# One-hot matrices in the place of one weight slot, row transposes done later, and outputs stored by halves of the tokens

## The chip, the cores and the metric

The kernel runs on one core of a Trainium2 chip. The metric is the time of one execution in device microseconds (us); lower is better. Engines are named as the profile names them: PE (TensorE matmuls), PEld (TensorE weight loads), DVE (VectorE), ACT (ScalarE), POOL (GpSimd), SP (the queue that issues the weight transfers). A small q behind a name means the engine's sequencer.

## The reference, cut to what matters

Two layers of a diffusion backbone on 256 latent and 256 context tokens of width 1024. After its mixer each layer has a mixture of experts: a router picks 2 of 16 experts for every token, and the experts' results come back to their tokens, weighted by the gates:

```
idx, gates = route(tokens, router_w, router_b)          # 2 of 16 experts a token
for e in range(16):                                     # SwiGLU, 1024 -> 768 -> 1024
    y_e = (silu(h[tok_e] @ w_gate[e]) * (h[tok_e] @ w_up[e])) @ w_down[e]
    y[tok_e] += gate_e * y_e
x = layer_norm(alpha * x + m[5] * y)
```

Layer 0 does this for all 512 tokens, layer 1 for the 256 latent ones. The weights of one expert are 9.4 MB in float32 and are read from DRAM for each layer, 16 experts times 2 layers. The output is the latent stream, 256 x 1024.

## The kernel before

Activations lie feature-major in SBUF (128 partitions x 8 feature tiles x tokens). A residual sum `acc` (`self.acc`) takes every sub-layer's result; the layer norm of the next stage reads it.

**Weights and slots.** Expert weights come in chunks of 1536 KB: four for gate and up (`gu`, from `in_egu`) and two for down (`ed`, from `in_ed`), six an expert. A chunk lands in a slot of 12 KB a partition. Layer 0's experts have ten slots: three of `ring`, four in `big`, three of `more` (`R1, R2, R3`, L39; `open_slots`, L1448). `wload` (L334) takes the slot at the head of a list and puts it back at the tail, so load number n takes the slot that load n-10 had, and SP issues it when PE has made its last use of that one. The order of loads is gu(0), then gu(e), ed(e-1) for e from 1 on. Two slots are also held until the first gather of tokens has been issued (`self.held`, L1458).

**The expert loop** (L1766) runs over e from 0 to 15; p = e // 2 is the pair, m = e % 2. Step e puts on PE, in this order: `hidden` of expert e (`gu0p` in the trace: 128 matmul instructions for the first 64 tokens, one run-time branch each for tokens 65 to 96 and 97 to 128), for odd e the `features` of the next pair (`xt0p`), then `down` of expert e-1 (`dp0p`). PE's own order is kept as written (`self.pin`), except for the blocks under a run-time branch (`when`, L1488). The results of both experts of a pair are put in one tile Y.

**How results come back to the tokens in layer 0.** There are two ways. Pairs 0 to 5 (`NS = 6`) scatter their rows to DRAM (`scatter`, L1600, on POOL): four planes, one for each 256 features, with two rows a token, one for each of its two experts. When pair 5 is scattered, at e = 12, `fetch(0)` (L1612) reads the rows of the 256 context tokens back on POOL's queue in 16 transfers into a tile `rows0` and adds the two rows of each token on POOL, in two halves of 128 tokens (L1620). `collect(got, 0)` (L1624) transposes these rows on PE (16 matrices of 128 x 128, `cl` in the trace), and DVE adds them to `acc` (8 instructions, L1597). `fetch(1)` and `collect(got, 1)` do the same for the latent rows. Pairs 6 and 7 don't go through DRAM: `combine` (L1634) makes one-hot matrices on DVE (L1593; 8 of 128 x 512 in layer 0), multiplies Y by them on PE (`cm0p`), and DVE adds the products to `acc` (16 instructions). The rows tile and the one-hot tile share one buffer, tag `rb`, so they take turns.

In the kernel before, `collect(got, 0)` stands at the end of step 13 (behind `down` of expert 12) with `fetch(1)` behind it, and `collect(got, 1)` at the end of step 14 (behind `down` of expert 13; L1806). `combine` of pair 6 is in the middle of step 15, `down` of expert 15 and `combine` of pair 7 follow the loop. Then come a branch on the fullest expert (L1850), the last modulation of layer 1 (`ada(1, 1)`) and layer 1.

**The end.** `finish` (L398) normalizes the latent stream in two halves of 128 tokens, side by side. Each half adds its bias in place and stores its tiles in two transfers of 256 KB (L411); in `out` the 128 tokens of one feature and half are 512 bytes in a row.

Of the kernel before, what the change touches and what calls it, by code (L numbers as in the profile page):

```python
# [21 lines left out]
D = 1024  # L22
# [13 lines left out]
WIN = 128, 96  # L36

NS = 6
R1, R2, R3 = 3, 4, (3, 5)  # L39

EARLY, LATE = (1, 0), (4, 1)
AREA_SLOTS = ((0, 3072, 6144, 9216), (6144, 0, 3072, 9216))
# [237 lines left out]
class Core:  # L280
# [117 lines left out]
    def finish(self):  # L398
        nc = self.nc
        self.act_table(LNEXP)  # L400
        g, b = self.lnp(1, 1)

        def then(x, rs, ts):
            for k in range(KT):
                nc.vector.scalar_tensor_tensor(x[:, k], x[:, k], g[:, k:k + 1], rs, op0=OP.mult, op1=OP.mult)  # L405
                if ts.start and k % 4 > 1:
                    nc.vector.tensor_scalar(x[:, k], x[:, k], b[:, k:k + 1], None, op0=OP.add)  # L407
                else:
                    self.act(x[:, k], x[:, k], AF.Identity, bias=b[:, k:k + 1])
                if k % 4 == 3:  # L410
                    nc.sync.dma_start(self.O['out'][:, k - 3:k + 1, ts], x[:, k - 3:k + 1])  # L411
        together(self.layer_norm(1, 'fin', self.area_mem(1), 'ab', then, 128))


# [1033 lines left out]
    def open_slots(self, l):  # L1448
        more = [(self.pm, R3[l])] if l == 0 else [(self.pm, R3[l] - 3), (self.sp, 3)]
        more = [(p.tile([128, n * RING], F32, tag='more', name=f'more{l}{n}'), n) for p, n in more]  # L1450
        free = [self.big[:, o:o + RING] for o in AREA_SLOTS[l]] + [t[:, i * RING:(i + 1) * RING] for t, n in more for i in range(n)]
        now = self.rest[:len(free)]
        for i, t in zip(now, free):
            self.chunks[i] = t
        n = EARLY[l]
        self.slots = now[:n] + self.slots + now[LATE[l]:]
        self.late = now[n:LATE[l]]
        self.held = set(now[R2 - 2:R2] if l == 0 else [])  # L1458
        self.xg = [self.pm.tile([128, D], F32, name=f'xg{l}{i}') for i in range(2)]
        self.rows = self.dram.tile([T >> l, D], F32, name=f'rows{l}')  # L1460

# [17 lines left out]
    def experts(self, l, nb, pm, rows, xg, zero, pos, number, aux):  # L1479
# [89 lines left out]
        def features(nm, rv, xe, parts=(0, 1), G=None):  # L1569
            for S in parts:  # L1570
                x = self.spare('xe', S) if l else pm.tile([128, 1024], F32, tag=f'xe{S}', name=f'xe{l}{nm}{S}')
                x = x.rearrange('p (k s) -> p k s', k=KT)
                xe.append(x)
                p = [self.ps(f'xt{l}{nm}{S}{c}') for c in range(2)]

                def t_mm():
                    for k in range(KT):
                        if G:
                            for j in range(nb):
                                self.mm(p[k // 4][:, (k % 4) * 128:(k % 4 + 1) * 128], xg[j][:, k * 128:(k + 1) * 128], G[S][:, j],  # L1580
                                        start=k % 4 == 0 and j == 0, stop=j == nb - 1)
                            continue
                        self.tr(p[k // 4][:, (k % 4) * 128:(k % 4 + 1) * 128], xg[S][:, k * 128:(k + 1) * 128])
                if S == 0:
                    t_mm()
                else:
                    when(rv, 64, t_mm, lambda: [z_mm(p[c], 512) for c in range(2)])
                for c in range(2):
                    self.act(x[:, 4 * c:4 * c + 4], p[c].rearrange('p (k s) -> p k s', k=4), AF.Copy)
            return xe  # L1590

        def onehot(o, tok, i, S, q):
            nc.vector.tensor_scalar(o, self.C('iota')[:, :tn], tok[:, q, i, S:S + 1], None, op0=OP.is_equal)  # L1593
            return o
# [17 lines left out]
        def fetch(a):  # L1612
            rb = pm.tile([128, 2, 2, D], F32, tag='rb', name=f'rows{a}')
            for j in range(2):
                for i in range(2):
                    for q in range(4):
                        o = i * T + a * TC + j * 128
                        nc.gpsimd.dma_start(rb[:, j, i, q * 256:(q + 1) * 256], self.planes[q][o:o + 128])
            for j in range(2):
                nc.gpsimd.tensor_tensor(rb[:, j, 0], rb[:, j, 0], rb[:, j, 1], op=OP.add)  # L1620
            return rb[:, :, 0]


        def collect(got, a):  # L1624
            for c in range(KT // 2):
                p = self.ps(f'cl{l}{a}{c}', 'b')
                for k in range(2 * c, 2 * c + 2):
                    for j in range(2):
                        o = (k % 2) * TC + j * 128
                        self.tr(p[:, o:o + 128], got[:, j, k * 128:(k + 1) * 128])  # L1630
                for k in range(2 * c, 2 * c + 2):
                    add(k, a, p[:, (k % 2) * TC:(k % 2 + 1) * TC])

        def combine(nm, Y, tok, i, rv):  # L1634
            o = pm.tile([128, 8, tn], F32R, tag='rb', name=f'oh{l}{nm}')
            oh = {(S, q): onehot(o[:, 4 * S + q], tok, i, S, q) for q in range(4) for S in range(2)}
            for qh in range(2):
                ps = [self.ps(f'cm{l}{nm}{qh}{dd}', 'b') for dd in range(4)]

                def part(S, dd):  # L1640
                    for h in range(2):
                        self.mm(ps[dd][:, :tn], Y[S][h][:, qh, dd * 128:(dd + 1) * 128], oh[S, 2 * qh + dd // 2],
                                start=S == 0 and h == 0, stop=S == 1 and h == 1)
                for dd in range(4):
                    part(0, dd)
                when(rv, 64, lambda: [part(1, dd) for dd in range(4)])
                for dd in range(4):
                    for a in range(nb // 2):
                        add(4 * qh + dd, a if l == 0 else 1, ps[dd][:, a * TC:(a + 1) * TC])
# [46 lines left out]
        def transposed(nm, H):  # L1696
            hT = pm.tile([128, 4, 192], F32, tag='hT', name=f'hT{l}{nm}')[:, :nt]
            nc.vector.transpose(hT.rearrange('p t s -> p (t s)'), H.rearrange('p t s -> p (t s)'))  # L1698
            return hT
# [41 lines left out]
        def count(i):  # L1741
            return nc.tensor.value_load(cnt[0:1, i:i + 1], min_val=0, max_val=T)
# [23 lines left out]
        for e in range(NE):  # L1766
            p, m = divmod(e, 2)
            if m == 0:
                xe, ((idx, tok, gt, to), i) = nxt, info[p]
                ti = i - (NS - 2 if i else 0)  # L1770
                full = count(NE + p)
                if 0 < p < NP - 1:
                    gathers(p + 1)
            rv = count(e)
            W = load_gu(e)
            Wd = load_d(e - 1) if e else None

            def between():
                if e == 0:
                    features('p0', full, xe, (1,), G0)  # L1780
                    some_lists(1, 1)
                    gathers(1)
                if m == 1 and pend:
                    combine(*pend)

            def middle():
                if last:
                    last[2] = transposed(*last[2])
            H = hidden(f'p{p}{m}', m, xe, gt, i, W, rv, middle, between)
            if m == 1 and p + 1 < NP:  # L1790
                if l and p + 2 < NP:
                    some_lists(p + 2, 1)
                nxt = features(f'p{p + 1}', count(NE + p + 1), [])
            if m == 1:
                Y = outputs(f'p{p}', 1 + (p >= ns))
            if last:
                down(*last[:3], Wd, last[3], Y)
            pend = None
            if m == 0 and e:
                if p > ns:  # L1800
                    pend = (f'p{p - 1}', Y, *was[:3])
                else:
                    scatter([y[0] for y in Y], *was[3:])
                    if p == ns:
                        got = fetch(0)
            if ns and 1 <= e - 2 * ns <= 2:  # L1806
                collect(got, e - 2 * ns - 1)
                if e == 2 * ns + 1:
                    got = fetch(1)
            last, was = [f'p{p}{m}', m, (f'p{p}{m}', H), rv], (tok, ti, full, to, i, NE + p)  # L1810
            if e == 1 and l == 0:
                some_lists(2, NP - 2)
        down(*last[:2], transposed(*last[2]), load_d(NE - 1), rv, Y)
        combine(f'p{NP - 1}', Y, tok, ti, full)
        self.pin = False

# [55 lines left out]
```

## Time and profile before

| | us |
|---|---|
| median of 3 runs | 1479.63 |
| lowest to highest | 1478.18 to 1479.75 |
| the profiled execution's own time | 1476.77 |
| its span, first to last instruction | 1475.0 |

| engine | busy us | share of the span |
|---|---|---|
| PE | 1244.8 | 84% |
| DVE | 682.9 | 46% |
| ACT | 396.8 | 27% |
| POOL | 141.9 | 10% |

In the trace layer 0's experts run from 396.58 us (first `gu0p`) to 851.82 us (last `cm0p`). A matmul counts as busy from its issue to its modelled end, so neighbours overlap, and a busy share near 100% does not mean that no faster order exists. The granted clock is a share of full speed: 1.00 is 2.4 GHz, about 0.5 is 1.2 GHz. A "releaser" is what ended an engine's idle time; "issue" means that the trace shows no semaphore that did.

### The profile page before, as it was taken

The numbers are of one execution on the slowest core, as the hardware profiler recorded it, in microseconds if no ns is written. First come the engines' busy times: TensorE is split into PE (matmuls) and PEld (weight loads), VectorE is DVE, ScalarE is ACT, GpSimd is POOL, SyncE is SP. The second block draws the span as 40 slices with busy tenths as digits, with TensorE's granted clock in tenths as the row PEclk, the third lists the DMA queues.
The fourth block names the chain that finished last, engine by engine and source line by source line (L and its number), as shares of the span: only waits on it lengthen the run. The fifth ranks groups of instructions, "written<-read, shape, count | busy, mean of one in ns | idle before, by whom it ended". The sixth has DMA issues, their size and how long they took to land. (4 is left out here: it accounts for less than half of the span.)

```text
span 1475.0 us, 27640 instructions
## 1 busy us (share of the span) xinstructions
PE 1244.8 (84%) x11433; PEld 735.0 (50%) x11434; DVE 682.9 (46%) x1777; ACT 396.8 (27%) x787; POOL 141.9 (10%) x153
## 2 busy tenths in 40 slices
PE   4899989899589799999859777998968688898775
PEld 0597553577334345554424435876834444454333
DVE  1847436875524121011214468737765245454435
ACT  1633234344210110111111134434431122121223
POOL 0000010201200211021133002002010000000000
PEclk8899998899699999999989988999989898998996
DMA  9431578225478999789999441274388899999981
GB/s 341 167 116 43 204 312 353 73 81 206 173 287 341 375 389 419 309 329 423 420 413 361 160 159 44 100 271 157 129 334 355 373 419 425 425 425 422 425 379 32
DMA packets 49474, 411.85 MB, mean 279 GB/s; under 512 B 7195, under 2 KB 11439, under 8 KB 18064
## 3 DMA queue, kind: packets, MB, share of 16 engines
q1 hardware_dynamic: 41200, 388.40, 64.8%
q0 software_dynamic: 7232, 17.71, 3.3%
q8 instruction: 139, 2.28, 0.6%
q10 hardware_dynamic: 864, 3.15, 0.5%
q14 instruction: 39, 0.32, 0.1%
HBM read 402.02 MB, written 13.11 MB: 281 GB/s over the span
## 5 line engine op out<-in xcount | busy, mean ns | idle before, releaser
L1670 DVE SCALAR_TENSOR_TENSOR h0p<-gu0p,gt0p,sg0p 128x192 f32<-128x192 f32 x64 | 25.3, 415 | 176.4 <-ACT sg0p L321 175.9
L345 PE MATMUL gu1p<-more,big 128*32 128x384 f32 x976 | 85.4, 493 | 7.8 <-issue 2.9
L345 PE MATMUL gu0p<-big,xe0p 128*32 128x384 f32 x992 | 89.8, 487 | 0.8 <-issue 0.6
L321 ACT ACTIVATE sg0p<-gu0p 128x192 f32<-128x192 f32 x64 | 19.7, 332 | 247.8 <-PE gu0p L345 244.6
L345 PE MATMUL ada<-ring,small 128*32 128x512 f32 x344 | 63.9, 700 | 19.6 <-DMA ring<-in_ada 14.9
L345 PE MATMUL gu0p<-ring,xe0p 128*32 128x384 f32 x768 | 75.5, 505 | 0.7 <-ACT sg0p L321 0.5
L345 PE MATMUL gu0p<-more,xe0p 128*32 128x384 f32 x800 | 75.0, 494 | 0.5 <-issue 0.5
L1670 DVE SCALAR_TENSOR_TENSOR h1p<-gu1p,gt1p,sg1p 128x192 f32<-128x192 f32 x48 | 20.0, 416 | 115.9 <-ACT sg1p L321 115.8
L345 PE MATMUL dp0p<-big,hT0p 128*32 128x256 f32 x792 | 57.6, 394 | 6.3 <-issue 3.8
L345 PEld LDWEIGHTS gu1p<-more,big 128*32 128x32 f32 x976 | 39.1, 110 | 47.0 <-issue 36.9
L321 ACT ACTIVATE big<-big 128x512 f32<-128x512 f32 (+2 forms) x81 | 44.5, 575 | 64.6 <-DVE big L646 29.2
L321 ACT ACTIVATE y1p<-dp1p 64x512 fp32r<-64x512 f32 x64 | 37.9, 592 | 81.4 <-PE dp1p L345 79.8
L345 PEld LDWEIGHTS gu0p<-big,xe0p 128*32 128x32 f32 x992 | 39.4, 110 | 40.9 <-issue 34.2
L321 ACT ACTIVATE y0p<-dp0p 64x512 f32<-64x512 f32 (+1 forms) x40 | 23.7, 592 | 130.7 <-PE dp0p L345 102.3
L321 ACT ACTIVATE sg1p<-gu1p 128x192 f32<-128x192 f32 x48 | 15.9, 331 | 154.5 <-PE gu1p L345 140.1
L345 PE MATMUL zo<-zo,zw 128*128 128x256 f32 x384 | 56.2, 297 | 0.0
L1603 POOL DMA_INDIRECT plane<-y0p,to0p x36 | 35.6, 988 | 204.3 <-ACT y0p L321 176.9
L345 PEld LDWEIGHTS zo<-zo,zw 128*128 128x128 f32 x384 | 50.1, 197 | 6.6 <-issue 4.3
L345 PEld LDWEIGHTS <-zero 128*128 128x128 bf16 x105 | 10.0, 97 | 86.1 <-issue 67.0
L345 PE MATMUL gu1p<-big 128*32 128x384 f32 x528 | 52.2, 509 | 0.0
L345 PE MATMUL dp0p<-ring,hT0p 128*32 128x256 f32 x624 | 46.7, 389 | 5.2 <-issue 4.9
L345 PE MATMUL dp1p<-ring,hT1p 128*32 128x256 f32 x576 | 43.9, 455 | 4.4 <-DVE hT1p L1698 2.6
(559 smaller groups left out, 2422.2 us busy)
## 6 DMA issues: line engine op xcount, KB each, us to landing
more<-in_egu SPq DMA_DIRECT2D x54, 1536.0 KB, 16.0
big<-in_egu SPq DMA_DIRECT2D x48, 1536.0 KB, 16.7
ring<-in_ada SPq DMA_DIRECT2D x27, 1536.0 KB, 8.2
ring<-in_ed SPq DMA_DIRECT2D x27, 1536.0 KB, 12.8
ring<-in_egu SPq DMA_DIRECT2D x26, 1536.0 KB, 14.0
big<-in_ed SPq DMA_DIRECT2D x21, 1536.0 KB, 11.5
more<-in_ed SPq DMA_DIRECT2D x16, 1536.0 KB, 14.8
ring<-in_odw SPq DMA_DIRECT2D x5, 1536.0 KB, 6.1
```

What stands on the lines that cost most here:

```text
L321: a = self.nc.scalar.activation(out, x, func, **kw)
L345: i = self.nc.tensor.matmul(out, lhsT, rhs, start=start, stop=stop, skip_group_check=True)
L1603: nc.gpsimd.indirect_dma_start(out=self.planes[q], out_offset=bass.IndirectOffsetOnAxis(ap=to[:, q, i, S:S + 1], axis=0), in_=Y[S][:, q // ...
L1670: nc.vector.scalar_tensor_tensor(H[:, t], p[:, 192:384], gt[:, 2 * m + t % 2, i, t // 2:t // 2 + 1], sg, op0=OP.mult, op1=OP.mult)
```

## The change

Three things change. (1) Layer 0 has two `more` slots in the place of three, so nine slots in all; the freed 12 KB a partition become a tile `onehots` of six one-hot matrices, which `combine` uses in turn in layer 0. In both layers the one-hots are made four at a time, ahead of each half of the features, and no longer eight at once. (2) `collect(got, 0)` and `fetch(1)` move from the end of step 13 into step 14, behind `hidden` of expert 14 and ahead of `down` of expert 13; `collect(got, 1)` moves from step 14 to behind `down` of expert 15, ahead of the last `combine`. The `rb` buffer is now the rows' alone in layer 0. (3) `finish` writes its biased result to a tile of its own at `big` 8192, and `out` is laid out by halves, so that one partition's four feature tiles of a half are 2 KB in a row.

```
-R1, R2, R3 = 3, 4, (3, 5)
+R1, R2, R3 = 3, 4, (2, 5)
 # finish
+            h = ts.start // 128
+            y = self.place(8192 + 1024 * h, [128, KT, 128])
-                    nc.vector.tensor_scalar(x[:, k], x[:, k], b[:, k:k + 1], None, op0=OP.add)
+                    nc.vector.tensor_scalar(y[:, k], x[:, k], b[:, k:k + 1], None, op0=OP.add)
-                    self.act(x[:, k], x[:, k], AF.Identity, bias=b[:, k:k + 1])
+                    self.act(y[:, k], x[:, k], AF.Identity, bias=b[:, k:k + 1])
-                    nc.sync.dma_start(self.O['out'][:, k - 3:k + 1, ts], x[:, k - 3:k + 1])
+                    nc.sync.dma_start(self.O['out'][:, h, k - 3:k + 1], y[:, k - 3:k + 1])
 # open_slots
+        if l == 0:
+            self.ohs, self.noh = self.pm.tile([128, 6, T], F32R, name='onehots'), 0
 # combine
-            o = pm.tile([128, 8, tn], F32R, tag='rb', name=f'oh{l}{nm}')
-            oh = {(S, q): onehot(o[:, 4 * S + q], tok, i, S, q) for q in range(4) for S in range(2)}
+            o = pm.tile([128, 8, tn], F32R, tag='rb', name=f'oh{l}{nm}') if l else None
+            def place(S, q):
+                if l:
+                    return o[:, 4 * S + q]
+                self.noh += 1
+                return self.ohs[:, self.noh % 6]
             for qh in range(2):
+                oh = {(S, q): onehot(place(S, q), tok, i, S, q) for q in range(2 * qh, 2 * qh + 2) for S in range(2)}
 # the expert loop, behind hidden(e) and the next pair's features
+            if ns and e == 2 * ns + 2:
+                collect(got, 0)
+                got = fetch(1)
...
-            if ns and 1 <= e - 2 * ns <= 2:
-                collect(got, e - 2 * ns - 1)
-                if e == 2 * ns + 1:
-                    got = fetch(1)
...
         down(*last[:2], transposed(*last[2]), load_d(NE - 1), rv, Y)
+        if ns:
+            collect(got, 1)
         combine(f'p{NP - 1}', Y, tok, ti, full)
```

## Rows read from the trace of the kernel before

**Rows 1.** The page: span, busy time of PE, DMA share in 40 slices.
```profile
span 1475.0 us, 27640 instructions
...
PE 1244.8 (84%) x11433; PEld 735.0 (50%) x11434; DVE 682.9 (46%) x1777; ACT 396.8 (27%) x787; POOL 141.9 (10%) x153
...
DMA  9431578225478999789999441274388899999981
```
**Rows 2.** PE's waits, 430 to 852 us: us in total, times, longest.
```profile
PE dp0p L345 <- issue: 14.1, 10, 2.8
PE gu0p L345 <- issue: 13.5, 7, 4.8
PE cl L350 <- POOL rows L1620: 11.8, 1, 11.8
```
**Rows 3.** Timeline of PE at the collects: start, us, instructions, idle before and releaser.
```profile
760.44 1.27 PE L345 MATMUL dp0p<-more,hT0p 128*32 128x256 f32 x17 [1.54 <-issue]
761.64 0.33 PE L350 MATMUL cl<-const,rows 128*128 128x128 f32 x1
773.73 2.61 PE L350 MATMUL cl<-const,rows 128*128 128x128 f32 x11 [11.76 <-POOL rows L1620]
776.27 2.78 PE L345 MATMUL gu0p<-more,xe0p 128*32 128x384 f32 x14
...
798.82 1.97 PE L350 MATMUL cl<-const,rows 128*128 128x128 f32 x16
```
**Rows 4.** Timeline of POOL: last row transfer, second add, `fetch(1)` and its last add.
```profile
758.52 0.54 POOL L1618 DMA_DIRECT2D rows<-plane  x1 [0.53 <-DMA rows<-plane]
...
771.34 2.34 POOL L1620 TENSOR_TENSOR rows<-rows 128x1024 f32<-128x1024 f32 x1 [9.90 <-DMA rows<-plane]
780.50 8.48 POOL L1618 DMA_DIRECT2D rows<-plane  x16 [6.83 <-PE cl L350]
...
796.00 2.38 POOL L1620 TENSOR_TENSOR rows<-rows 128x1024 f32<-128x1024 f32 x1 [4.61 <-issue]
```
**Rows 5.** Windows: length; PE, PEld, DVE, ACT, POOL busy; granted clock; DMA share; GB/s.
```profile
761.97:773.73 11.76, 0.00 (x1) 0.01 (x1) 0.75 (x1) 0.96 (x2) 2.34 (x1) 0.53 1.02 418
773.73:780.00 6.27, 6.27 (x33) 3.62 (x37) 3.82 (x9) 0.00 (x0) 0.00 (x0) 0.53 0.89 375
780.00:790.64 10.64, 10.48 (x120) 3.99 (x122) 1.29 (x3) 0.33 (x1) 10.13 (x17) 1.00 0.74 236
...
800.70:812.20 11.50, 11.50 (x130) 4.26 (x130) 7.44 (x18) 0.33 (x1) 0.00 (x0) 1.00 1.00 421
```
**Rows 6.** Timeline of SP's issues: ed(13), ed(14).
```profile
752.30 0.33 SPq L338 DMA_DIRECT2D ring<-in_ed  x1
...
787.95 0.81 SPq L338 DMA_DIRECT2D more<-in_ed  x2
```
**Rows 7.** Line 338's landing times, 702.4 to 703.3 us.
```profile
DMA to landing us min/median/max: 9.6/11.2/12.7
```
**Rows 8.** Timeline of PE, where these two chunks, ed(11), are first used.
```profile
721.72 1.46 PE L345 MATMUL dp0p<-big,hT0p 128*32 128x256 f32 x19
...
725.18 1.05 PE L345 MATMUL dp0p<-ring,hT0p 128*32 128x256 f32 x10
```
**Rows 9.** Timeline of PE in the last combine of layer 0.
```profile
844.38 3.23 PE L345 MATMUL cm0p<-oh0p,y0p 128*128 128x512 f32 x7 [0.93 <-DVE y0p L1735]
848.76 3.06 PE L345 MATMUL cm0p<-oh0p,y0p 128*128 128x512 f32 x8 [1.15 <-DVE big L1597]
```
**Rows 10.** Timeline of DVE there.
```profile
847.74 3.23 DVE L1597 SCALAR_TENSOR_TENSOR big<-cm0p,mods,big 128x256 f32<-128x256 f32 x8 [3.42 <-PEq L1492]
```
**Rows 11.** Groups of DVE instructions, 430 to 852 us: busy us, mean ns, idle before.
```profile
L1593 DVE TENSOR_SCALAR oh0p<-const,tok0p 128x512 fp32r<-128x512 f32 x16 | 6.7, 480 | 0.0
```
**Rows 12.** The page's DMA issues: KB each, median us to landing.
```profile
out<-big SPq DMA_DIRECT2D x4, 256.0 KB, 3.2
...
ring<-in_odw SPq DMA_DIRECT2D x1, 512.0 KB, 3.3
```

More of the change, by code (lines that the diff above doesn't have):

```diff
@@ L1865 @@
     ins = {k: nc.dram_tensor(f'in_{k}', list(a.shape), mybir.dt.from_np(a.dtype), kind='ExternalInput').ap() for k, a in arrays.items()}
-    out = nc.dram_tensor('out', [128, KT, TC], F32, kind='ExternalOutput')
+    out = nc.dram_tensor('out', [128, 2, KT, 128], F32, kind='ExternalOutput')
     build(nc, ins, {'out': out.ap()})
@@ L1870 @@
     y = r.results[0]['out']
-    return np.ascontiguousarray(y.transpose(2, 1, 0).reshape(1, TC, D))
+    return np.ascontiguousarray(y.transpose(1, 3, 2, 0).reshape(1, TC, D))
```

## The prediction

> **What bounds the kernel now.** Read the page first: PE is busy for 84% of 1475.0 us, DVE for 46%, and the DMA line stands mostly at 9 in layer 0's experts (the 14th to the 22nd of 40 slices) and again in layer 1's from the 33rd on [rows 1]. So in layer 0 it is PE or the weights, and the change touches both: a PE wait (the collects) and a weight slot. Next PE's list of waits in that stage [rows 2]: no entry is released by a weight transfer, so weights arrive in time, and PE's order sets the stage's length. Its longest single wait is one of 11.8 us for POOL's rows at `collect(got, 0)`; the other large entries, 14.1 and 13.5 us, are 17 short waits for nothing that the trace shows. Third, the two timelines around that wait. PE has the first `cl` transpose done at 762 us, idles 11.76 us, and goes on at 773.73 [rows 3]; POOL's last row transfer is issued at 758.52, its second add can start only at 771.34 and ends at 773.68 [rows 4]. PE is in order, so `hidden` of expert 14 (the `gu0p` from 776.27 on) stands behind it, although its weights were issued before 752.30, ahead of ed(13) [rows 6].
>
> **The change, part by part.**
>
> *The wait goes: -11.8 us.* `collect(got, 0)` now stands behind `hidden`(14). PE leaves `down`(12) at 761.7 [rows 3] and can start `hidden`(14) at once. At the full clock such a stage takes 11.5 us (that of expert 15, 800.70 to 812.20 [rows 5]), so PE comes to the transposes at about 761.7 + 11.5 = 773.2. The rows are ready at 773.68: the fetch is issued as before and meets the same weight traffic up to 758.52. That leaves 0.5 us. If the row transfers landed sooner it would be 0; if the last of them took as long again as the half of its 12.8 us (758.52 to 771.34), 6. I take 0.5, since nothing ahead of it changes.
>
> *The slow clock behind the wait goes: -3.5 us.* The granted clock is 0.53 in the wait and up to 780.00, that is 1.2 GHz, and 1.00 after it [rows 5]. From 773.73 to 790.64, 16.9 us, PE does `hidden`(14) and 15 of 16 transposes. At the full clock that is 11.5 + 15/16 x 1.97 (the second collect's 16, [rows 3]) = 13.4 us. 16.9 - 13.4 = 3.5. With PE busy from 761.7 on, nothing makes the clock fall there. If some of it stays, it is at worst 3.5.
>
> *The second collect moves into the tail of the layer: 0.* Its 1.97 us on PE at 798.82 go [rows 3]. Behind `down`(15) they come back, partly in PE's wait for Y's eviction (the first row of [rows 9] waited 0.93 us for DVE). But its eight adds (8 x about 0.41 us by the row of eight in 3.23 us, [rows 10]) free the PSUM tiles that the last `combine` fills, behind Y's eviction on DVE. DVE was idle 3.42 us there before its adds [rows 10], so most of the 3.2 us has a place; the first `combine` tile waits for two adds, 0.8 us, and each later one for two more, as fast as PE fills them (8 instructions in 3.23 us). Bounds: +0.8 us if they fit in the gap, +4.0 if all stand ahead (0.8 + 3.2). I take +2.0, nearer to the gap; with -2.0 that is 0, from -1.2 to +2. POOL's rows for it are no matter: `fetch(1)` took from 780.50 to 798.38 [rows 4], starts earlier now, and is wanted some 50 us later.
>
> *Six one-hot places in the place of eight: +0.7 us.* A one-hot costs 0.48 us on DVE [rows 11], 16 as before. The first four and two of the second four have free places and can be made ahead, as all eight are now. The last two of each `combine` wait until PE has read the first two, and in DVE's queue they can fall behind the eight adds of the first half; behind them stand the adds of the second, and PE waits for both. PE's second half is paced by those adds anyway (848.76 waits for DVE [rows 9]), so between 0 and 2 x 0.48 = 1 us for each of two combines, and as much again if the adds behind are late: 0 to 3. I take 0.7. In layer 1 all eight have places as before: 0, at most 4 x 0.48 = 1.9 in its last `combine`.
>
> *Nine slots: 0.* Load n now waits for the slot of load n-9, that is for the release that load n+1 had. Mostly this is the next of four chunks, freed at the same time; the fourth gate-and-up chunk, though, waits for the end of the `hidden` before its own, and SP's queue is in order (what stands behind it, ed, is freed at the same moment). For expert 14 that is the moment when ed(13) was issued, 752.30 [rows 6]. By the 12.7 us of the slowest chunk of [rows 7] it lands at 765, and is wanted as the fourth quarter of `hidden`(14), at 761.7 + 3/4 x 11.5 = 770. The tightest other pair is ed(11): issued by 703.3 and landed within 12.7 us, by 716.0 [rows 7]; first used at 721.72 and 725.18 [rows 8]. One slot less lets each land one chunk later; at 418 to 421 GB/s [rows 5] 1536 KB take 3.75 us, so 719.8 against 721.72 at worst. Close, but not late. With PE 15 us ahead in steps 14 and 15, ed(14), issued at 787.95 at the end of `hidden`(14), moves with it to about 773 and is wanted behind the `combine` of pair 6, over 30 us later. Bounds: 0, and a chunk late in each of three tight steps, 3 x 3.75 = 11. I take 0, as no row shows PE waiting for a weight.
>
> *Outputs in rows of 2 KB: -0.2 us.* Only the last store stands on the path. A 256 KB store lands in 3.2 us, a 512 KB read with longer rows in 3.3 [rows 12]; less 256 KB at 420 GB/s (0.6 us) that is 2.7. So 0 to -0.5; -0.2. The Trainium skill (DMA: Bandwidth & Descriptors, Specifications) puts the size from which a transfer runs at line rate at 512 B, which the old rows have; by it this term would be 0. The separate tile adds no instruction, and the weights that lay there were read before the norm began.
>
> *Sum.* -11.8 + 0.5 - 3.5 + 0 + 0.7 + 0 - 0.2 = -14.3 us. Layer 1 begins when layer 0's sums are done, and its weights wait for slots that its own steps free, so all of it moves up together. The profiled execution took 1476.77; 1476.8 - 14.3 = 1462.5. The median of the runs is 2.9 us above that, so 1479.6 - 14.3 = 1465.3.
>
> **The rivals.**
>
> *The rows come late at the new place.* For it: POOL waited 9.90 us for the last transfers [rows 4] with the DMA share at 1.02 [rows 5]. Against: up to 758.52 the same transfers are under way. With the 6 us from above, and half of the slow clock back (1.8): 1465.3 + 7.3 (less the 0.5 counted) = about 1473. Chance 8%.
>
> *Branch waits move.* The 17 waits without a releaser, up to 4.8 us each, 27.6 us in all [rows 2], stand among run-time branches, and moving 16 transposes with their weight loads shifts what lies behind them. Two such waits more or fewer, 2 x 4.8: 1455.7 or 1475. Against: nothing says which way. Chance 10%, half to each side. The Trainium skill (Runtime: NRT & Kernel Launch, Instruction fetch mechanics) says that a taken branch out of the loaded pages must fetch before execution goes on, and that straight code hides its fetches; by that rule such waits depend on where the code lies. No row here shows where a page ends.
>
> *Slower: the weights run late with nine slots.* Where the DMA line is full, a chunk that PE waits for costs 3.75 us a step, and an idle PE loses clock besides, 3.5 us for a wait of 11.8 [rows 5], or 0.3 us for each us. For it: 1.9 us of cover are left at ed(11) by the worst landing. Against: the median landing of [rows 7] is 11.2 us, and [rows 2] has no weight wait with ten slots. It decides from the third late step on: 3 x 3.75 x 1.3 = 14.6 is the whole gain. Eight late steps, those of experts 7 to 14, cost 39 us: 1504. Chance 7%, of which 2% are a tie at three.
>
> *The transposes stay where they were.* A run-time block may be put elsewhere in PE's order, but the transposes are kept in theirs. If not, only the stores' 0.2 us and the one-hots' 0.7 remain: 1480. Chance 3%.
>
> **How the numbers follow.** Forecast 72%, at 1465.3. With the small terms at their good ends it gains 11.8 + 3.5 + 1.2 + 0.5 = 17.0 us, at their bad ones 11.8 - 0.5 + 3.5 - 2 - 3 - 1.9 = 7.9: 1462.6 to 1471.7. Taking in the late rows at 1473 and the bad side of the branches at 1475, and a part of their good side, 1459.5 to 1475 holds it 8 times in 10; the slower case, the last rival and the rest of the good side, 15%, are left out, and some for the unforeseen. About 0.2%, 3 us, is what a measurement here tells from no change. Faster by more: 72 + 8 + 10 = 90%, less 2 for what I have not thought of, 88. Within 0.2%: the 3% of the last rival, the tie's 2% and 1: 6. Slower: 5 and 1: 6.
>
> **What would show it.** Right: no `cl` wait above 1 us on PE; the granted clock at 1.00 from 760 to 780; `gu0p` of expert 14 starting at about 762; layer 0's last `cm0p` ending near 851.8 - 14 = 838; the same distance from there to the end. Wrong: a PE wait with a weight transfer as releaser; `hidden`(14) starting with an idle PE ahead of it; more than 2 us between `down`(15) and `combine` than before; new waits without releaser longer than 5 us.

## The result, and the profile after

| | before | after |
|---|---|---|
| median of 3 runs, us | 1479.63 | 1458.05 |
| lowest to highest | 1478.18 to 1479.75 | 1457.82 to 1460.23 |
| the profiled execution's own time | 1476.77 | 1460.23 |
| its span | 1475.0 | 1458.2 |

The ratio is 0.9898, with a 95% interval of 0.9862 to 0.9933. It is not the quotient of the two medians, which lie 21.6 us apart (0.9854); with three runs on each side these are loose. Two later comparisons on other chips, with 6 and 8 runs of the changed kernel against 23 and 16 of the kernel before, gave 0.9929 (0.991 to 0.9949) and 0.9917 (0.989 to 0.9945). So the kernel is 0.7 to 1.0% faster. The forecast was 14.3 us of 1479.6, a ratio of 0.9903, and a median of 1465.3 us.

Read the page first, against [rows 1]: 16.8 us less span, 7.5 us less busy PE, and the DMA line is as full as before.

```profile
span 1458.2 us, 27643 instructions
...
PE 1237.3 (85%) x11433; PEld 732.8 (50%) x11434; DVE 684.0 (47%) x1777; ACT 398.1 (27%) x787; POOL 142.8 (10%) x153
...
DMA  9331578215469999789999542273388899999991
```

Then PE's waits in layer 0's experts, 430 to 852 us (us in total, times, longest), against [rows 2]. The wait for POOL's rows is gone, and no weight transfer has come into the list. The waits without a releaser ("issue") went down under `gu0p` and up under `dp0p`; with two of 1.4 us under `xt0p` and `sl0p` they sum to 26.4 us, where it was 27.6.

```profile
PE dp0p L345 <- issue: 18.9, 11, 3.8
PE gu0p L345 <- DVE h0p L1682: 6.0, 7, 1.1
PE ada L345 <- PEq L1863: 4.8, 1, 4.8
PE gu0p L345 <- issue: 4.7, 4, 2.3
```

Next PE's timeline at the first collect, against [rows 3]. `hidden`(14) starts behind `down`(12) with no gap, and the transposes start at 775.50 with none. But two stops of 2.30 and 1.68 us have appeared, the one in the last quarter of `hidden`(14), the other in `down`(13).

```profile
758.76 1.27 PE L345 MATMUL dp0p<-ring,hT0p 128*32 128x256 f32 x17 [1.63 <-issue]
759.65 5.54 PE L345 MATMUL gu0p<-more,xe0p 128*32 128x384 f32 x64
...
768.12 1.48 PE L345 MATMUL gu0p<-ring,xe0p 128*32 128x384 f32 x10
771.90 3.67 PE L345 MATMUL gu0p<-ring,xe0p 128*32 128x384 f32 x22 [2.30 <-issue]
775.50 2.66 PE L350 MATMUL cl<-const,rows 128*128 128x128 f32 x16
...
783.01 1.28 PE L345 MATMUL dp0p<-ring,hT0p 128*32 128x256 f32 x19 [1.68 <-issue]
...
788.25 0.49 PE L345 MATMUL gu0p<-big,xe0p 128*32 128x384 f32 x1
```

The windows answer to [rows 5] (length; busy time of PE, PEld, DVE, ACT, POOL; granted clock; DMA share; GB/s). The clock is at 2.4 GHz up to the stop and at 1.2 GHz for 3.4 us behind it; before, it was low for 18 us.

```profile
759.65:771.90 12.25, 9.95 (x114) 5.86 (x107) 2.36 (x3) 1.19 (x2) 2.38 (x1) 1.00 1.01 419
772.35:775.76 3.41, 3.41 (x23) 1.08 (x15) 0.42 (x1) 0.48 (x2) 0.00 (x0) 0.50 1.01 425
776.00:790.00 14.00, 12.11 (x176) 7.14 (x178) 6.25 (x14) 2.37 (x6) 5.88 (x11) 1.00 1.01 418
```

POOL's timeline, against [rows 4]: the first fetch's second add ends at 767.6, 6 us sooner than before and 8 us before PE comes. The second fetch begins 1.8 us sooner than before (778.70) but takes 34 us to the end of its last add, 812.8, where it took 18.

```profile
765.23 2.38 POOL L1625 TENSOR_TENSOR rows<-rows 128x1024 f32<-128x1024 f32 x1 [9.25 <-issue]
778.70 4.26 POOL L1623 DMA_DIRECT2D rows<-plane  x8 [11.09 <-PE cl L350]
...
810.41 2.37 POOL L1625 TENSOR_TENSOR rows<-rows 128x1024 f32<-128x1024 f32 x1 [10.32 <-DMA rows<-plane]
```

The DMA view of 770 to 830 us says why: GB/s in 40 slices of 1.5 us, and the landing time of the second fetch's 16 transfers. First the kernel before:

```profile
GB/s 396 434 442 434 396 352 221 101 240 254 224 257 298 336 418 382 442 421 418 434 418 451 393 434 426 426 434 418 150 33 52 238 418 374 442 434 158 8 106 254
...
rows<-plane POOLq DMA_DIRECT2D x16, 128.0 KB, 3.2
```

and after:

```profile
GB/s 410 426 451 401 434 426 453 385 448 388 432 382 418 382 445 374 432 380 418 404 418 393 396 421 418 404 421 434 434 412 410 431 393 257 49 8 30 284 49 3
...
rows<-plane POOLq DMA_DIRECT2D x16, 128.0 KB, 12.7
```

Before, PE's stall had let the weight traffic run dry (the seventh to the fourteenth number; SP issued no weight load between 761.74 and 787.95), and the second fetch ran through that lull. Without the stall there is none, and a transfer of 128 KB lands in 12.7 us instead of 3.2.

The tail of layer 0, against [rows 9, 10]: the end of `down`(15), the second collect and `combine`.

```profile
823.32 2.32 PE L345 MATMUL dp0p<-ring,hT0p 128*32 128x256 f32 x34 [1.05 <-issue]
825.57 1.97 PE L350 MATMUL cl<-const,rows 128*128 128x128 f32 x16
827.29 0.48 PE L345 MATMUL cm0p<-onehots,y0p 128*128 128x512 f32 x1
828.49 0.49 PE L345 MATMUL cm0p<-onehots,y0p 128*128 128x512 f32 x1 [0.72 <-DVE y0p L1747]
829.49 2.27 PE L345 MATMUL cm0p<-onehots,y0p 128*128 128x512 f32 x6 [0.51 <-DVE big L1602]
832.91 3.05 PE L345 MATMUL cm0p<-onehots,y0p 128*128 128x512 f32 x8 [1.15 <-DVE big L1602]
```

From the end of `down`(15) to the end of the last `combine` is now 835.97 - 825.64 = 10.33 us with the collect in it; it was 851.82 - 841.65 = 10.17 without, from this end of `down`(15):

```profile
838.85 2.80 PE L345 MATMUL dp0p<-ring,hT0p 128*32 128x256 f32 x23
```

And the stores, against [rows 12]:

```profile
out<-big SPq DMA_DIRECT2D x4, 256.0 KB, 2.7
```

### The profile page after: what moved, and what is told of

Read it like the earlier page. It is cut to its first block, busy times and chain, and to the rows that moved or that the text cites. A ratio compares the mean times of both kernels' runs of the same rounds, so it can differ in the third digit from the quotient of the medians.

```text
span 1458.2 us, 27643 instructions
## 1 busy us (share of the span) xinstructions
PE 1237.3 (85%) x11433; PEld 732.8 (50%) x11434; DVE 684.0 (47%) x1777; ACT 398.1 (27%) x787; POOL 142.8 (10%) x153
## 3 DMA queue, kind: packets, MB, share of 16 engines
q8 instruction: 139, 2.28, 0.6%
## 5 line engine op out<-in xcount | busy, mean ns | idle before, releaser
L345 PE MATMUL gu0p<-big,xe0p 128*32 128x384 f32 x1040 | 97.8, 487 | 0.5 <-issue 0.3
L345 PE MATMUL gu0p<-ring,xe0p 128*32 128x384 f32 x832 | 82.9, 498 | 2.5 <-issue 2.3
L345 PE MATMUL dp0p<-big,hT0p 128*32 128x256 f32 x912 | 72.5, 394 | 7.4 <-issue 6.1
L345 PE MATMUL ada<-ring,small 128*32 128x512 f32 x332 | 59.0, 667 | 16.7 <-DMA ring<-in_ada 16.7
L345 PE MATMUL gu0p<-more,xe0p 128*32 128x384 f32 x688 | 64.7, 487 | 0.5 <-ACT sg0p L321 0.5
L345 PEld LDWEIGHTS gu0p<-big,xe0p 128*32 128x32 f32 x1040 | 43.4, 110 | 42.0 <-issue 36.0
L345 PE MATMUL dp0p<-ring,hT0p 128*32 128x256 f32 x720 | 54.4, 381 | 7.6 <-issue 5.6
L345 PEld LDWEIGHTS gu1p<-more,big 128*32 128x32 f32 x976 | 34.9, 110 | 51.7 <-issue 44.7
L321 ACT ACTIVATE sg1p<-gu1p 128x192 f32<-128x192 f32 x48 | 15.9, 332 | 156.6 <-PE gu1p L345 142.2
L345 PEld LDWEIGHTS gu0p<-ring,xe0p 128*32 128x32 f32 x832 | 35.2, 111 | 35.4 <-issue 31.8
L345 PEld LDWEIGHTS dp0p<-big,hT0p 128*32 128x32 f32 x912 | 36.9, 112 | 30.9 <-issue 17.1
## 6 DMA issues: line engine op xcount, KB each, us to landing
ring<-in_egu SPq DMA_DIRECT2D x28, 1536.0 KB, 11.8
big<-in_ed SPq DMA_DIRECT2D x23, 1536.0 KB, 15.8
```

The costliest lines, as they stand in the source:

```text
L321: a = self.nc.scalar.activation(out, x, func, **kw)
L345: i = self.nc.tensor.matmul(out, lhsT, rhs, start=start, stop=stop, skip_group_check=True)
```

## The experiments

Each ratio is to runs of the kernel before on the same chip. The medians of the kernel before there were 1472.9 to 1474.4 us.

**e1_full_again: the changed kernel once more.** 

> The changed kernel again, for a closer figure than the first three runs gave (the profiled executions differ by 16.5 us, the medians by 21.6 us, the ratio with its interval by 10 to 20 us). Theory A (the collect's wait and the slow clock behind it are the gain; branch waits that moved give some of it back): 14 to 18 us below the kernel before, a ratio of 0.988 to 0.990. If the medians were the truth, 21 us below, 0.9855. The trace repeats the first one's: no wait on PE for POOL's rows, the last combine of layer 0 ends about 16 us earlier.

1461.34 us, ratio 0.9929 (0.991 to 0.9949): less than the 0.988 to 0.990 that was expected. The two stops on PE's timeline stand again at the same instructions, 2.28 and 1.68 us long, but the clock behind the first is 1.00 here (768.71 to 772.10): the same 22 matmuls take 2.14 us and not 3.67.

```profile
768.71 2.14 PE L345 MATMUL gu0p<-ring,xe0p 128*32 128x384 f32 x22 [2.28 <-issue]
...
778.29 1.28 PE L345 MATMUL dp0p<-ring,hT0p 128*32 128x256 f32 x19 [1.68 <-issue]
```

**e2_nine_slots: the kernel before with one slot less.**

```
-R1, R2, R3 = 3, 4, (3, 5)
+R1, R2, R3 = 3, 4, (2, 5)
```

> The kernel before with one thing of the change, nine slots in the place of ten; the freed 12 KB stay empty, collects, one-hots and outputs are those of before. Theory A, and the prediction's term of 0 for the slot: the time of before within 2 us, no PE wait for a weight, the collect's wait of 11 to 12 us still there. Rival B (the weights run late with nine slots): a chunk of 3.75 us in each of three or more tight steps, 11 us or more slower, with weight transfers named among PE's waits.

1484.81 us, ratio 1.0075 (1.0056 to 1.0094): slower. No weight is late: the largest PE wait with a weight transfer as releaser in the experts is 0.2 us. PE's timeline shows that the time is lost 400 us earlier, ahead of the experts. The 192 products of the attention's output, which stood among the scores before, come in one piece behind them; the first norm starts 15.8 us later (342.36 against 326.57).

```profile
317.67 24.77 PE L345 MATMUL zo<-zo,zw 128*128 128x256 f32 x192 [3.77 <-ACT zw L321]
```

So either a slot has a price that the forecast missed, or the 12 KB that fell out moved something else.

**e3_no_move: the changed kernel with the collects at their old places.**

```
-            if ns and e == 2 * ns + 2:     # behind hidden(14)
-                collect(got, 0)
-                got = fetch(1)
+            if ns and 1 <= e - 2 * ns <= 2:     # at the end of steps 13 and 14
+                collect(got, e - 2 * ns - 1)
+                if e == 2 * ns + 1:
+                    got = fetch(1)
...
-        if ns:
-            collect(got, 1)
```

> The whole change without the move of the collects: nine slots, six one-hot places, the new outputs, but both collects and the second fetch where they were before. Theory A: within 2 us of the kernel before, less about 0.2 us for the stores, so 1477 to 1481 where before has 1479.6, with the wait of 11 to 12 us and the clock at 1.2 GHz behind it. If the gain came from the one-hots' own tile or the outputs, this one would have it: 10 us or more below before.

1473.99 us, ratio 0.9998 (0.9979 to 1.0017). Without the move nothing is gained, and nine slots, the one-hots' own tile and the outputs together cost nothing that can be measured.

**e4_new_outputs: the kernel before with the new stores alone** (the output's layout and the tile of its own). 

> The kernel before with the new outputs alone: a tile of its own for the biased result and rows of 2 KB in the output. The prediction's term: 0 to 0.5 us faster, 0.2 taken; by the first trace of the changed kernel the last store lands about 0.5 us sooner and the distance from the last instruction to the end is 0.14 us shorter, so 0.1 to 0.5. Rival C (the 1.1 us that the changed kernel gained after its last combine came from the outputs): 1.0 us or more below before.

1472.44 us, ratio 0.9997 (0.998 to 1.0013): within what can be told from nothing. The landing time did not do what was expected of it: in this kernel the new stores land later than the old ones, in 3.7 us against the 3.2 of [rows 12].

```profile
out<-big SPq DMA_DIRECT2D x4, 256.0 KB, 3.7
```

**e5_nine_kept: one slot less, the space kept.**

```
-R1, R2, R3 = 3, 4, (3, 5)
+R1, R2, R3 = 3, 4, (2, 5)
...
+        if l == 0:
+            self.pm.tile([128, 6, T], F32R, name='onehots')     # never used
```

> The kernel before with nine slots, the freed 12 KB a partition taken by a tile that nothing reads or writes, so that every other tile stays at its address. Theory: the slot itself costs nothing, and the 11 us of e2_nine_slots came from the tiles behind it moving up, which put the 192 products of the attention's output behind the scores in PE's order (24.77 us at 317.67) instead of among them. Then: ratio 1.000 within 0.002, scores and output products interleaved as before, no PE wait with a weight transfer as releaser. Rival: one slot less delays weights or shifts the order by itself: ratio 1.005 to 1.009 again, with the products in one piece.

1472.49 us, ratio 1.0013 (0.999 to 1.0035), and the products stand among the scores again. The slot costs nothing that can be measured; what cost e2_nine_slots 11 us was the empty space. In what way the tiles' places set PE's order there was not followed.

**e6_ten_moved: the move without the one-hots' own tile.** With one buffer for rows and one-hots, the second collect has to come before the `combine` of pair 6.

```
-            if ns and 1 <= e - 2 * ns <= 2:
-                collect(got, e - 2 * ns - 1)
-                if e == 2 * ns + 1:
-                    got = fetch(1)
+            if ns and e == 2 * ns + 2:     # behind hidden(14)
+                collect(got, 0)
+                got = fetch(1)
...
                 if m == 1 and pend:
+                    if ns:
+                        collect(got, 1)
                     combine(*pend)
```

> The kernel before with the move alone: ten slots, one-hots and rows still in one buffer, so the second collect has to stand ahead of the combine of pair 6, in the middle of hidden(15). Theory: the wait of 11.8 us at the first collect goes here too; the rows of the second fetch take 18 us from about 778 and are ready at about 796, as PE arrives, and the first one-hot (0.48 us each) can only be made when the last transpose has read the buffer, with eight adds (3.2 us) in DVE's queue: combine of pair 6 some 3 to 5 us later than in the changed kernel. So 3 to 5 us slower than the changed kernel, ratio 0.994 to 0.997. Rival: the tenth slot is worth more than the one-hots' own place: ratio below 0.992.

1481.21 us, ratio 1.0046 (1.0029 to 1.0062): slower than the kernel before, a miss for both expectations. The whole wait is back, only at the second collect. Its rows were expected at 796 from the 18 us of [rows 4]; with weights flowing a transfer landed in 12.6 us and the rows were there at 811.3. PE's timeline and the landing time:

```profile
811.32 1.76 PE L350 MATMUL cl<-const,rows 128*128 128x128 f32 x7 [11.83 <-POOL rows L1620]
...
816.55 8.56 PE L345 MATMUL cm0p<-oh0p,y0p 128*128 128x512 f32 x32 [1.45 <-DVE oh0p L1593]
```

```profile
rows<-plane POOLq DMA_DIRECT2D x16, 128.0 KB, 12.6
```

**e7_shifted: 32 idle matmuls ahead of the experts.**

```
+        if l == 0:
+            p = self.ps('pad', 'b')
+            for _ in range(32):
+                z_mm(p, 128)
         nxt, last, Y, pend = ...
```

> The changed kernel with 32 more matmuls of zeros (weight load and matmul of 128 x 128 each, some 3 us) on PE ahead of layer 0's experts, while PE waits for the router and the gather; nothing else changes. Theory: PE's waits without a releaser hang on where the code lies behind run-time branches, so a shift of 64 instructions moves them: other places and lengths than the 2.30 us in hidden(14) and 1.68 us in down(13) that both profiles of the changed kernel show, a sum that differs from 26 us by 3 to 10 us either way, and a time that differs from the changed kernel's by about as much (ratio 0.986 to 1.000). Rival: they belong to the branches themselves: same places, same lengths, sum within 2 us, and a time within 3 us of the changed kernel's.

1468.31 us, ratio 0.997 (0.9949 to 0.999), 0.4 to 0.5% (6 to 8 us) above the changed kernel's 0.9929 and 0.9917. The places moved, as the theory said: the stop in `hidden`(14) is 1.46 us and stands ahead of a matmul of zeros (at 774.18), that in `down`(13) is gone, others are new. Their sum did not move by 3 to 10 us: it is 24.4, 2.0 less than in the changed kernel, which is as much as the rival allowed. But waits put down to PE's sequencer (the third line) rose from 0.8 to 6.1 us. The same work at other addresses thus makes some 0.4% of difference, part of it behind the stage that the change touches.

```profile
PE dp0p L345 <- issue: 14.2, 8, 3.0
PE gu0p L345 <- issue: 10.2, 5, 3.8
...
PE dp0p L345 <- PEq L1497: 6.1, 3, 3.3
```

**e8_second_in_15: the second collect between `hidden`(15) and `down`(14).**

```
             if ns and e == 2 * ns + 2:
                 collect(got, 0)
                 got = fetch(1)
+            if ns and e == 2 * ns + 3:
+                collect(got, 1)
...
-        if ns:
-            collect(got, 1)
         combine(f'p{NP - 1}', Y, tok, ti, full)
```

> The changed kernel with the second collect between hidden(15) and down(14), not behind down(15). Theory: in the tail its 1.97 us of transposes hide almost wholly in PE's waits for evictions (the last combine took 10.33 us with them against 10.17 without), so ahead of down(14) they cost their 1.6 to 2 us and the last combine, freed of them and of eight adds, gives back 0 to 2: the time 0 to 2 us above the changed kernel's or the same, the last combine 8.2 to 10.2 us long. Rival, the +2.0 us of the forecast: the eight adds in the tail do cost 2 us, and without them the last combine ends 2 us earlier, 8 us long, and the whole gains 0 to 2.

1468.69 us, ratio 0.9955 (0.9933 to 0.9977). A wait that neither theory had: PE stands 3.72 us for the second rows, as in e6_ten_moved. The tail answers the question asked: from the end of `down`(15), 830.42, to the end of the last `combine`, 840.58, it is 10.16 us without the collect, against 10.33 with it. So 16 transposes and eight adds in the tail cost 0.2 us and not 2.

```profile
811.83 2.57 PE L350 MATMUL cl<-const,rows 128*128 128x128 f32 x15 [3.72 <-POOL rows L1625]
...
825.09 5.33 PE L345 MATMUL dp0p<-ring,hT0p 128*32 128x256 f32 x86 [0.18 <-PEq L1497]
...
837.53 3.05 PE L345 MATMUL cm0p<-onehots,y0p 128*128 128x512 f32 x8 [1.15 <-DVE big L1602]
```

**e9_first_at_old: the first collect back, the second stays in the tail.**

```
-            if ns and e == 2 * ns + 2:     # behind hidden(14)
+            if ns and e == 2 * ns + 1:     # at the end of step 13
                 collect(got, 0)
                 got = fetch(1)
```

> The changed kernel with the first collect and the second fetch back at their old place, behind down(12); only the second collect stays in the tail, behind down(15). Theory: the wait at the first collect (10 to 12 us) returns and with it the lull in the weight traffic, so the second fetch's transfers land in about 3 us again and not in 12.7; what is left is the second collect, whose 1.97 us on PE go and come back as 0.2 us in the last combine: 1.8 us, ratio 0.997 to 1.000. Rival: much of the gain came from the second collect or from where the code lies, not from the first collect's wait: ratio 0.993 to 0.996 with the wait still there.

1468.57 us, ratio 0.9967 (0.9941 to 0.9993), on the border of the two expectations; the interval doesn't part them. The trace has what the theory said: the wait, and a second fetch that lands quickly again.

```profile
PE cl L350 <- POOL rows L1625: 10.2, 1, 10.2
```

```profile
rows<-plane POOLq DMA_DIRECT2D x16, 128.0 KB, 3.1
```

**e10_first_later: the first collect one block later, behind `down`(13).** The same three lines as in e9_first_at_old, with `e == 2 * ns + 2` at the end of the step. 

> The changed kernel with the first collect and the second fetch one block later still, behind down(13) at the end of step 14. Theory: the first collect has no wait left to save, but the second fetch starts some 9 to 11 us later, at about 785 to 789, in full weight traffic (its transfers land in about 12.7 us, 34 us in all), so its rows are ready at 820 to 823, just before PE wants them behind down(15) at about 822 to 825: a wait at the second collect of 0 to 3 us, ratio 0.992 to 0.996. Rival: the second fetch finds the queue free, as in the kernel before (18 us in all): ready at 804, no wait, ratio 0.991 to 0.994.

1457.34 us, ratio 0.9899 (0.9848 to 0.995), below both expectations, with an interval that reaches into both. The second fetch's last add ends at 813.60 + 2.35 = 815.95 on POOL, 34 us behind its start again, and PE comes for the rows at 818.29: no wait, with 2.3 us in hand.

```profile
813.60 2.35 POOL L1625 TENSOR_TENSOR rows<-rows 128x1024 f32<-128x1024 f32 x1 [9.56 <-DMA rows<-plane]
```

**e11_changed_5 and e12_later_5: the changed kernel and that of e10_first_later side by side.** 

> The changed kernel, on the same chip as e12_later_5, to settle its size. Two comparisons gave 0.990 and 0.993. Theory: the same on every chip, near the 14.3 us of the working (0.9903): ratio 0.989 to 0.993. Rival: the 3.5 us of the slow clock and some of the branch waits don't stay: 0.992 to 0.996.

> The kernel of e10_first_later once more, beside the changed kernel. Theory: neither collect waits in either kernel, so both do the same work on PE and differ by code places only: within 3 us of e11_changed_5, ratio 0.989 to 0.993. Rival: PE's first stop, some 0.5 us at the rows in two other kernels, and the slow clock behind it are gone for good: 3 to 6 us faster than e11_changed_5.

1460.81 us, ratio 0.9917 (0.989 to 0.9945), and 1460.82 us, 0.9915 (0.9886 to 0.9944): the same. The later place is no better, and e10_first_later's 1457.34 lies within the scatter. The size is settled only to the interval: the forecast's 0.9903 lies in it.

## Why the prediction was right, and where it was not

**The wait of 11.8 us: right.** It is gone in every kernel that moves the first collect and 9.7 to 11.8 us long in every one that doesn't. The 0.5 us left over was 0, because the first fetch ended 6 us sooner; in other runs of the same order 0.5 and 1.3 us did remain (e8_second_in_15, e6_ten_moved).

**The slow clock of 3.5 us: half right.** "With PE busy from 761.7 on, nothing makes the clock fall there" failed, since PE was not busy throughout, and with it the sign "granted clock at 1.00 from 760 to 780": it was 0.50 from 772.35 to 775.76. From the end of `down`(12) to the start of `hidden`(15) the forecast had 11.8 + 3.5 - 0.5 + 1.97 (the second collect gone from there) = 16.8 us less. Measured: 800.72 - 761.71 = 39.0 before and 788.25 - 760.03 = 28.2 after (the last row of the timeline above; eight matmuls of `down`(13) are issued behind it, so this border is good to some 0.5 us), 10.8 less. The missing 6 is in four of its rows: the new stops of 2.30 and 1.68, and 3.67 + 2.66 us of work that ran at 1.2 GHz for the most part and takes 2.14 + 1.97 at 2.4 GHz, 2.2 less.

**Where these stops come from.** The forecast took "branch waits move" for luck with no sign. It has one at this place: all eight profiles with the first collect behind `hidden`(14) or later have a stop without a releaser in the last quarter of that stage, 2.0 to 2.6 us long (1.46 at another instruction in e7_shifted). None of the six with the collect at its old place has one of over 1 us anywhere in the 30 us behind the wait, and the work there is the same.

What PE stops for can be read from the DMA view of the changed kernel. The stop of 2.30 us begins at 769.60 and that of 1.68 at 781.33. The windows 769.3 to 769.6 and 780.3 to 780.6 show one packet of the instruction queue each, that is, of program code (packets, MB, share of the window):

```profile
q8 instruction: 1, 0.02, 22.4%
q8 instruction: 1, 0.02, 22.1%
```

Nearly all such stops go with one. All 14 profiles together have 152 stops of 1 us or more without a releaser between 430 and 852 us, and 135 of them end 1.2 to 1.75 us behind the end of a 16 KB packet of this queue. By chance it would be one in 13, as these stretches make up 8% of the time. So most of these stops are waits for code. Most packets bring no stop: there are 812 of them. The Trainium skill (Runtime: NRT & Kernel Launch, Instruction fetch mechanics) says that fetching runs on by itself while the code goes straight and that a taken branch outside the loaded window stops for a fetch. The trace agrees that code comes in as the kernel runs and that PE stops for some of it; that a taken branch stands ahead of each stop it does not show. The stops repeat from run to run and move with the code (e1_full_again, e7_shifted).

Why the kernels with the long wait have none there is open. The wait did not load code ahead: from 762 to 774 the profile before has no packet of this queue. But behind it PE ran at 1.2 GHz up to 780.00 and so came later to the code that it needed, the DMA traffic soon fell to 236 GB/s [rows 5], and the code of `hidden`(14) stood 16 transposes further on. No run parts these three. The place alone is the least likely: e7_shifted moves the code the other way, by twice as much, and has a stop there too.

**Other stops of this kind paid part of that back.** In the profile before, there is one of 1.75 us in `hidden`(15) and one of 2.16 us in `down`(15); in the profile after, the first is gone and the second is 1.05 us.

```profile
815.15 0.32 PE L345 MATMUL gu0p<-zero 128*128 128x384 bf16 x1 [1.75 <-issue]
...
836.74 0.42 PE L345 MATMUL dp0p<-ring,hT0p 128*32 128x256 f32 x3 [2.16 <-issue]
```

With this the stages from `hidden`(15) on gained 851.82 - 800.72 = 51.1 against 835.97 - 788.25 = 47.7, 3.4 us that the forecast didn't have. With 1.7 us won ahead of the first collect the sum at the end of layer 0 is 1.7 + 10.8 + 3.4 = 15.9, where the forecast had 14.1 (14.3 with the stores) for all of it. It is a sum of a right term, a missed cost and a lucky return. The kernel with the wait still in it (e5_nine_kept) had a span of 1467.2 us, 7.8 less than the kernel before, with a ratio of 1.0013 for the two: a difference between two single profiles is good to no more than some 5 to 8 us.

**The second collect in the tail: mis-sized, +2.0 for 0.2 us.** Its transposes stand where PE would wait for Y's eviction, and six of its eight adds fall between that eviction and the next adds, in DVE's gap (e8_second_in_15 against the changed kernel: 10.16 and 10.33). So the case "if they fit in the gap" was right, not the middle that was taken; its +0.8 was still too much, and with the 1.97 us that go elsewhere the whole term is -1.8, outside its bounds of -1.2 to +2.

**`fetch(1)`: harmless by luck of place.** "It starts earlier now, and is wanted some 50 us later" failed in its duration: 34 us and not 18, since the 18 belonged to the lull which the change removes (e9_first_at_old, where lull and short landing times are back). The slack was 825.57 - 812.8 = 12.8 us. Wanted at 808, PE waited 3.7 us and about half of the gain was lost (e8_second_in_15); wanted at 799, with one buffer for rows and one-hots, PE waited 11.8 us and all of it was lost and more (e6_ten_moved).

**Nine slots: right at 0,** within the intervals of e5_nine_kept and e3_no_move. No weight was late. The fourth chunk of expert 14's gate and up was issued at 750.83 and landed in 9.5 us, at 760.3, 8 us before its use. But the term holds only because the one-hots fill the space (e2_nine_slots).

**The six one-hot places and the stores.** Both are under what a run can tell. The tail leaves no room for the +0.7 of the one-hots beyond the 0.2 above; the ratio of e4_new_outputs is 0.9997. The 2.7 us of the profile after, which the forecast had for the stores, don't show that longer rows land sooner: over all profiles the old rows landed in 3.1 to 3.9 us (four kernels) and the new ones in 2.7 to 3.7 (ten), and the one that changes nothing else, e4_new_outputs, has 3.7. The rule that the forecast weighed there, a line rate from 512 B on (the Trainium skill, DMA: Bandwidth & Descriptors, Specifications), would make the term 0; nothing here speaks against it.

**Layer 1: right.** From the last `combine` to the end it took 623.2 us before and 622.2 after.

**What made the gain.** The move is all of it (e3_no_move), and the own tile for the one-hots is what makes it possible: the same first move without it loses 0.46% (e6_ten_moved). Of the two collects the second one's place is worth some 0.3% and the first one's 0.4 to 0.5% more (e9_first_at_old against the changed kernel), with intervals of 0.2 to 0.3% on each. For the first collect this is 6 to 7 us, give or take 5, where the forecast's terms for it come to 11.8 + 3.5 - 0.5 = 14.8. The timelines say the same: from the end of `down`(12) to the start of `hidden`(15), e9_first_at_old takes 796.04 - 761.35 = 34.7 us and the changed kernel 28.2, 6.5 less.

## What to carry to other kernels

A transfer's duration belongs to the traffic around it: before a wait is removed, ask which transfers ran in its shadow, and time them again at full load. A term read off a wait is an upper bound, because other waits can turn up once it is gone; here 4 of 15 us came back as PE's short stops for code, and 2 more as the slow clock behind one of them. And a freed tile is not free: test a size change with the space kept.

## What the runs showed of the hardware

A DMA of 128 KB from DRAM on POOL's queue landed in 3.1 to 4.3 us in the lull of the weight traffic (101 to 336 GB/s in all in the profile before; medians of the six kernels with the wait), and in 12.4 to 12.7 us beside full weight traffic of some 420 GB/s (the eight without). PE's stops without a releaser mostly end 1.2 to 1.75 us behind the end of a 16 KB packet of the instruction queue (135 of 152). 64 instructions of idle code (32 matmuls with their weight loads) far ahead of a stage moved stops of 1 to 3 us within it and behind it, at the price of some 0.4% of the whole (e7_shifted). And the same stop of 2.3 us is followed by 1.2 GHz in one run of a program (granted clock 0.50 from 772.35 to 775.76 in the first profile of the changed kernel) and by 2.4 GHz in another (1.00 in e1_full_again).
